# The latents' first norm moved to the end of the context's second group, and weight casts from GpSimd to ScalarE in both context groups

## Chip, cores and metric

The kernel runs on one core of a Trainium2 chip. The metric is device time in microseconds, the median of several executions; one further execution was profiled. VectorE is DVE in the rows, ScalarE ACT, GpSimd POOL, TensorE PE, and SP issues the DMAs.

## What is computed

A block of two layers on 512 latent tokens and 256 context tokens of width 1024, all in float32. Layer 0 mixes by two groups of gated linear recurrences (HGRN2-like "A", GLA-like "B"), both directions, the context first, its final state carried into the latents. Layer 1 is attention. Each has a SwiGLU feed-forward behind it. Cut to what matters here:

```python
u_lat = modulate(x_lat, ng[0], ml[0], ml[1])      # norm, scale and shift
u_ctx = modulate(x_ctx, ng[0], mc[0], mc[1])
a_lat, b_lat, ag_lat, bg_lat = rec_features(u_lat, ...)   # u @ w_in, split
a_ctx, b_ctx, ag_ctx, bg_ctx = rec_features(u_ctx, ...)
def prefix_scan(lat, ctx, reverse):
    o_c, s_c = chunk_gla(q_c, k_c, v_c, g_c, s0)  # the context
    o, _ = chunk_gla(q, k, v, g, s_c)             # the latents, from its state
```

## The kernel before

Activations lie transposed, features on the partitions, in tiles of 128 x 512. Every weight product runs on split operands: a weight block of 128 x 1024 is loaded (`raw`), cast to a high part (`whi`), and the low part is the difference (`wlo`); activations have the same two parts (`uh`, `ul`), and TensorE adds up high x high, high x low and low x high (L180 with the weight stationary, L190 to L192 with the activation stationary). A context product is 24 matmuls of 256 columns.

`wload` (L119 to L135) issues the load, the cast and the subtraction. Which engine casts and which subtracts is looked up in `cfg["hi"]` and `cfg["lo"]`, strings whose letters are used in turn: p for GpSimd (L130), a for ScalarE (L132), d for VectorE (L133); `engines(ph)` sets them for a phase, and a phase that is not in its table has p and d. `raw` has four buffers, `whi` and `wlo` three each.

The stretch of the change, in the order of the program:

- Phase `ra`: the first context group. `rec_group_a(SC, uc)` makes 12 products for group A's two gates and query (evacuated at L696 and L700); `rec_v_group` makes the values with four weight loads (evacuated at L756).
- Merged into its second half is `norm_lat0`, the latents' first norm: `pre_lat` loads x in eight tiles (L109), squares them on ScalarE (L348, L352), adds the squares on GpSimd (L353), makes the reciprocal root (L369 to L373), spreads it over the partitions by TensorE (L376) and multiplies (L611); `norm_mod` scales (L423), adds the shift and rounds to the high part on ScalarE (L424) and makes the low part (L408). These are the operands of all latents' projections.
- Phase `rb`: the second context group. The first product (for the gates of group B, L765 to L772), four products for B's query and key (L780), B's values, and the gates of the output (`rec_group_g`, L793), 17 weight loads. Merged into it are `gla_a(SC)`, the context's scan of group A, and `gla_b_feat(SC)`, the features of B's scan.
- Phase `la`: the latents' first group, merged with the context's scan of B, its output gates and products, and the weights of the modulation.

`gla_a` makes decays of the gates (L946 to L961; the running sum at L820) and then goes, for each direction and pair of chunks, through transposed keys (TensorE L845, ScalarE L847), scores (L223 into a `tr` bank, masked by VectorE at L873), key-value products (L223 into a `kv` bank), states (ScalarE L988 for the first, GpSimd L984, VectorE L990) and outputs (L223 into the one `o` bank, ScalarE L1001 and L1006, VectorE L1008). There are two `tr` and three `kv` banks.

`merge(main, side, ratio)` steps the side generator `ratio` times for each step of the main one. The order so written is a priority only: a scheduler then lays the instructions into each engine's queue, and a planner gives the buffers of the `u` pool. Each engine runs its queue in order.

Of the kernel before, what the change touches and what calls it, by code (L numbers as in the profile page):

```python
# [45 lines left out]
def block_kernel(ctx, tc, plan, xT, cT, vecs, w2, cst, atm, rope, ada, rec_a, rec_v, rec_g, rec_o, qk_w, v_w, wo_w, ff_in, ff_out, out):  # L46
# [17 lines left out]
    def ut(shape, dt=F32, name="u"):  # L64
        return slot(up, "u", shape, dt, name)
# [37 lines left out]
    SL, SC = Stream("l", NT_L), Stream("c", NT_C)  # L103
# [9 lines left out]
    def ch(tiles, st, k):  # L113
        return tiles[k // st.r][:, k % st.r, :]


    cfg = {"hi": "p", "lo": "d", "n": 0, "pri": 0, "evp": 150, "ll": False}
# [107 lines left out]
    def psg():  # L225

        t = rr["tags"][rr["i"] % len(rr["tags"])]
        rr["i"] += 1
        return ps(t)
# [230 lines left out]
    def new_u(st, alloc=None):  # L460
        return tuple([(alloc or ut)([P, st.r, st.nt], F32R, name="u" + n_) for _ in range(st.ntile)] for n_ in "hl")
# [78 lines left out]
    def engines(ph):  # L540
        cfg["pri"] = {}.get(ph, 200)
        cfg["ll"] = ph in []
        cfg["hi"], cfg["lo"] = {'co': ['a', 'ddp'], 'rb': ['p', 'ddp'], 'ci': ['a', 'd'], 'kv': ['a', 'ddp'], 'wo': ['pa', 'd'], 'l0': ['a', 'd'], 'f1': ['a', 'd'], 'lo2': ['p', 'dp'], 'kw': ['a', 'd']}.get(ph, ("p", "d"))

    def drain(*gens):
        for g in gens:
            for _ in g:
                pass

    def seq(*gens):  # L550
        for g in gens:
            yield from g
# [5 lines left out]
    def merge(main, side, ratio):  # L558

        acc = 0.0  # L560
        for _ in main:
            acc += ratio
            while acc >= 1.0:
                acc -= 1.0
                next(side, None)
            yield
        yield from side
# [28 lines left out]
    uc = new_u(SC)  # L596
# [54 lines left out]
    def norm_lat0():  # L651
        if XE == 0:
            yield from pre_lat()
        if 1:
            yield from norm_mod(xl0n, None, G1, ada0[0], 0, ul, FL, st=SL)
        else:
            yield from norm_mod(xl0, xl0n[0], G1, ada0[0], 0, ul, FL)
# [85 lines left out]
    def rec_v_group(st, g, u):  # L743
        f = feats[st.name]
        vs = [ut([P, 512], name="v") for _ in range(st.ntok)]
        if g == 0:
            f.vA = vs
        else:
            f.vB = vs
        for hf in range(2):  # L750
            wh = [wload(rec_v[g, hf, q], 1024) for q in range(2)]
            for tt in range(st.ntok):
                p_ = psg()[:, :256]
                gemm_b(p_, wh, u[0], u[1], st, tt)
                with tc.high_priority(offset=cfg["evp"]):
                    nc.scalar.copy(vs[tt][:, hf * 256 : hf * 256 + 256], p_)  # L756
                if tt % 2:
                    yield

    def rec_group_b(st, u):  # L760
        f = feats[st.name]
        lr = ut([32, st.nt], name="lr")
        p_ = proj_one(st, 16, u)
        with tc.high_priority(offset=cfg["evp"]):
            nc.scalar.copy(lr, p_[0:32])  # L765
        yield
        f.gx = [ut([P, st.r, st.nt], name="gxB") for _ in range(4 // st.r)]
        for h in range(4):
            p_ = psg()[:, : st.nt]
            mm(p_, w2s[:, h * 128 : (h + 1) * 128], lr, start=True, stop=True)  # L770
            with tc.high_priority(offset=cfg["evp"]):
                nc.scalar.activation(ch(f.gx, st, h), p_, AF.Identity, bias=vec("bg2", h, h + 1))  # L772
        yield
        f.qk = [[None, None], [None, None]]
        for s in range(2):
            for m in range(2):
                p_ = proj_one(st, 12 + 2 * s + m, u)
                f.qk[s][m] = ut([P, st.nt], name="qkB")
                with tc.high_priority(offset=cfg["evp"]):
                    nc.scalar.mul(f.qk[s][m], p_, 0.125 if s == 0 else 1.0)  # L780
                yield

    def rec_group_g(st, u):
        f = feats[st.name]
        f.gate = [[ut([P, 512], name="gate") for _ in range(st.ntok)] for _ in range(2)]
        for g in range(2):
            for hf in range(2):
                wh = [wload(rec_g[g, hf, q], 1024) for q in range(2)]
                for tt in range(st.ntok):
                    p_ = psg()[:, :256]  # L790
                    gemm_b(p_, wh, u[0], u[1], st, tt)
                    with tc.high_priority(offset=cfg["evp"]):
                        nc.scalar.copy(f.gate[g][tt][:, hf * 256 : hf * 256 + 256], p_)  # L793
                    if tt % 2:
                        yield
# [223 lines left out]
    def gla_b_feat(st):  # L1019
        f = feats[st.name]  # L1020
        n = st.nch
        qd, kd = [], []
        DL = base.tile([P, 4, n], F32, name=uid("dl"), tag=f"dlB{st.name}")
        BM = base.tile([P, 4, n], F32, name=uid("bm"), tag=f"bmB{st.name}")
        nt4 = 4 // st.r
        tl = [ut([P, st.r, st.nt], name="lsg") for _ in range(nt4)]
        for i in range(nt4):
            nc.scalar.activation(tl[i], f.gx[i], AF.Abs)
            nc.scalar.activation(tl[i], tl[i], AF.Exp, scale=-1.0)
        yield  # L1030
        for i in range(nt4):
            nc.scalar.activation(tl[i], tl[i], AF.Ln, bias=1.0)
        yield
        for i in range(nt4):
            nc.vector.scalar_tensor_tensor(b65(gpad[gi[0] % NG])[:, :, 1:65], v8(f.gx[i], st), 0.0, v8(tl[i], st),
                                           ALU.min, ALU.subtract)
            bx = scan_gate()
            a = ut([P, st.r, st.nt], name="aB")
            for d in range(2):
                i0, i1 = decay(bx, d, H[d])  # L1040
                nc.vector.tensor_sub(v8(a, st)[H[d]], i0, i1)
                edge(bx, d, H[d], flat8(DL, st, i), flat8(BM, st, i))
            q = ut([P, st.r, st.nt], name="EB")
            k = ut([P, st.r, st.nt], name="EiB")
            for r in range(st.r):
                h = i * st.r + r
                hp = H[h % 2]
                for d in range(2):
                    E = ut([P, st.nt], name="exB")[hp]
                    Ei = ut([P, st.nt], name="exiB")[hp]  # L1050
                    follow(gk(st), nc.scalar.activation(E, a[H[d], r, :], AF.Exp, scale=1.0 / 16.0))
                    follow(gk(st), nc.scalar.activation(Ei, a[H[d], r, :], AF.Exp, scale=-1.0 / 16.0))
                    nc.vector.tensor_mul(q[H[d], r, :], E, f.qk[0][h // 2][hp])
                    nc.vector.tensor_mul(k[H[d], r, :], Ei, f.qk[1][h // 2][hp])
            qd.append(q)
            kd.append(k)
            yield
        e = base.tile([P, n, 4], F32, name=uid("ex"), tag=f"exB{st.name}")
        ev = e.rearrange("p c h -> p h c")
        f0, f1 = H  # L1060
        nc.gpsimd.tensor_add(ev[f0, :, 1:n], DL[f0, :, 0 : n - 1], BM[f0, :, 1:n])
        nc.gpsimd.tensor_add(ev[f1, :, 0 : n - 1], DL[f1, :, 1:n], BM[f1, :, 0 : n - 1])
        if "B" in carry:
            D = carry["B"][1]
            nc.gpsimd.tensor_add(ev[f0, :, 0], D[f0, :, SC.nch - 1], BM[f0, :, 0])
            nc.gpsimd.tensor_add(ev[f1, :, n - 1], D[f1, :, 0], BM[f1, :, n - 1])
        else:
            nc.gpsimd.memset(ev[f0, :, 0], 0.0)
            nc.gpsimd.memset(ev[f1, :, n - 1], 0.0)
        nc.scalar.activation(e, e, AF.Exp, scale=1.0 / 16.0)  # L1070
        f.bfeat = (qd, kd, DL, e)
        yield
# [118 lines left out]
    if SH:  # L1191
        order = [(s, h) for s in [2, 0, 1] for h in range(4)]
        n1 = 8
        ga, rest = rec_group_a2(3, norm_lat0(), order, n1)
        drain(seq(ga, rec_v_group(SC, 0, uc)))
    else:
        rest = iter(())
        ga = rec_group_a(SC, uc)
        for i in range(6):
            cfg["pri"] = 0 if i < 4 else 0  # L1200
            next(ga)
        cfg["pri"] = 200
        drain(merge(seq(ga, rec_v_group(SC, 0, uc)), norm_lat0(), 0.7))
    rr["tags"] = ["mm"]
    engines("rb")
    rr["tags"] = ['mm']
    drain(merge(seq(rest, rec_group_b(SC, uc), rec_v_group(SC, 1, uc), rec_group_g(SC, uc)), seq(gla_a(SC), gla_b_feat(SC)), 2.8))
    engines("la")
    adat[0] = 'kv'
    rr["tags"] = ['mm', 'mm', 'kv']  # L1210
# [548 lines left out]
```

## Time and profile before

| | us |
|---|---|
| median of 3 runs (1813.05 to 1815.14) | 1813.13 |
| the profiled execution | 1816.63 |
| its span | 1814.8 |
| TensorE busy in it | 1735.1 |
| VectorE busy | 1067.6 |
| ScalarE busy | 751.0 |
| GpSimd busy | 441.4 |

The span goes from the first instruction to the last; the profiled execution has 1.8 us around it. Busy time of the engines overlaps. The mean granted clock of TensorE is 0.975 of its full level.

### The profile page before, as it was taken

How to read it: one execution, taken by the hardware profiler on the slowest of the kernel's cores; microseconds unless marked ns; L12 is line 12 of the kernel's file. 1: busy time of each engine (PE TensorE's matmuls, PEld its weight loads, DVE VectorE, ACT ScalarE, POOL GpSimd, SP SyncE). 2: the span in 40 equal slices, each digit the busy share in tenths (PEclk: the TensorE clock that was granted, in tenths of full speed). 3: DMA queues.
4: the chain of work that ended last, by engine and by line, in shares of the span. 5: the costliest groups of instructions: out<-in, count | busy, mean ns of one | idle time of the engine just before them, and what ended most of it. 6: DMA issues, size and time to landing. Idle time of an engine off the chain costs nothing. (4 is left out here: it accounts for less than half of the span.)

```text
span 1814.8 us, 27226 instructions
## 1 busy us (share of the span) xinstructions
PE 1735.1 (96%) x10711; PEld 1484.9 (82%) x10711; DVE 1067.6 (59%) x1717; ACT 751.0 (41%) x1314; POOL 441.4 (24%) x460
## 2 busy tenths in 40 slices
PE   6889999999899999999999999799999899999997
PEld 3877778798799989988888888787677898888886
DVE  4986544665777634798643536778855853322336
ACT  3653454344645544542222223434755552222311
POOL 3655412433331004400000002424444400000015
PEclk9989999999899999999999999899999899999999
DMA  9426557311144654576554423311011343233323
GB/s 338 136 86 188 174 180 236 93 49 57 47 140 124 179 171 131 189 252 216 182 162 148 139 73 108 112 37 59 12 48 47 117 129 99 86 94 113 97 66 113
DMA packets 83696, 228.18 MB, mean 126 GB/s; under 512 B 9296, under 2 KB 14160, under 8 KB 83568
## 3 DMA queue, kind: packets, MB, share of 16 engines
q1 hardware_dynamic: 83568, 226.45, 40.0%
q8 instruction: 84, 1.38, 0.3%
q14 instruction: 44, 0.36, 0.1%
HBM read 224.31 MB, written 2.10 MB: 125 GB/s over the span
## 5 line engine op out<-in xcount | busy, mean ns | idle before, releaser
L133 DVE TENSOR_TENSOR wlo<-raw,whi 128x1024 fp32r<-128x1024 f32 (+3 forms) x296 | 359.2, 1215 | 312.6 <-ACT whi L132 228.6
L132 ACT CAST whi<-raw 128x1024 fp32r<-128x1024 f32 (+2 forms) x199 | 201.5, 1014 | 467.3 <-issue 173.4
L130 POOL TENSOR_SCALAR whi<-raw 128x1024 fp32r<-128x1024 f32 (+1 forms) x113 | 121.1, 1074 | 762.3 <-PE ps_mm L180 356.8
L180 PE MATMUL ps_mm<-uh,whi 128*128 128x256 f32 (+1 forms) x840 | 289.3, 345 | 2.3 <-POOL whi L130 2.2
L180 PE MATMUL ps_mm<-uh,wlo 128*128 128x256 f32 (+1 forms) x840 | 286.2, 342 | 2.8 <-DVE wlo L133 2.8
L180 PE MATMUL ps_mm<-ul,whi 128*128 128x512 f32 (+1 forms) x840 | 287.1, 342 | 0.0
L180 PE MATMUL ps_kv<-uh,wlo 128*128 128x512 f32 (+1 forms) x696 | 246.0, 353 | 3.8 <-DVE wlo L133 3.8
L180 PE MATMUL ps_kv<-uh,whi 128*128 128x512 f32 (+1 forms) x696 | 247.7, 356 | 0.0
L180 PE MATMUL ps_kv<-ul,whi 128*128 128x512 f32 (+1 forms) x696 | 246.0, 353 | 0.0
L180 PEld LDWEIGHTS ps_mm<-uh,whi 128*128 128x128 f32 x840 | 161.3, 192 | 24.1 <-POOL whi L130 2.6
L180 PEld LDWEIGHTS ps_mm<-uh,wlo 128*128 128x128 f32 x840 | 160.8, 192 | 20.8 <-DVE wlo L133 3.1
L180 PEld LDWEIGHTS ps_mm<-ul,whi 128*128 128x128 f32 x840 | 161.2, 192 | 17.5 <-issue 0.5
L353 POOL TENSOR_TENSOR acc<-acc,sq 128x256 f32<-128x256 f32 (+1 forms) x79 | 93.4, 1185 | 261.9 <-ACT sq L352 255.8
L180 PEld LDWEIGHTS ps_kv<-uh,whi 128*128 128x128 f32 x696 | 132.7, 191 | 22.5 <-issue 2.9
L180 PEld LDWEIGHTS ps_kv<-uh,wlo 128*128 128x128 f32 x696 | 132.3, 190 | 21.8 <-DVE wlo L133 4.0
L180 PEld LDWEIGHTS ps_kv<-ul,whi 128*128 128x128 f32 x696 | 132.5, 190 | 17.6
L190 PE MATMUL ps_mm<-whi,uh 128*128 128x256 f32 x344 | 103.7, 302 | 8.4 <-ACT gate L793 8.4
L290 DVE SCALAR_TENSOR_TENSOR aacc<-ar,s,aacc 128x512 f32<-128x512 f32 x112 | 81.9, 759 | 34.0 <-DMA ar<-in_ada_dram 33.1
L191 PE MATMUL ps_mm<-wlo,uh 128*128 128x256 f32 x344 | 100.8, 295 | 0.7 <-DVE wlo L133 0.7
L192 PE MATMUL ps_mm<-whi,ul 128*128 128x256 f32 x344 | 100.5, 294 | 0.0
L180 PE MATMUL ps_kv<-hh,whi 128*128 128x512 f32 (+1 forms) x282 | 100.2, 355 | 0.0
L180 PE MATMUL ps_kv<-hh,wlo 128*128 128x512 f32 (+1 forms) x282 | 100.1, 355 | 0.0
(325 smaller groups left out, 3555.0 us busy)
## 6 DMA issues: line engine op xcount, KB each, us to landing
raw<-in_ff_in_dram SPq DMA_DIRECT2D x138, 512.0 KB, 3.7
ar<-in_ada_dram SPq DMA_DIRECT2D x192, 256.0 KB, 4.2
raw<-in_ff_out_dram SPq DMA_DIRECT2D x52, 512.0 KB, 3.5
raw<-in_rec_a_dram SPq DMA_DIRECT2D x34, 512.0 KB, 4.1
raw<-in_rec_v_dram SPq DMA_DIRECT2D x16, 512.0 KB, 3.7
raw<-in_rec_g_dram SPq DMA_DIRECT2D x16, 512.0 KB, 3.7
raw<-in_rec_o_dram SPq DMA_DIRECT2D x16, 512.0 KB, 3.6
raw<-in_wo_w_dram SPq DMA_DIRECT2D x14, 512.0 KB, 3.6
```

The lines of the kernel that those rows point to most:

```text
L130: nc.gpsimd.tensor_scalar(hi[:, :n], raw[:, :n], 1.0, 0.0, ALU.mult, ALU.add)
L132: nc.scalar.copy(hi[:, :n], raw[:, :n])
L133: (nc.gpsimd if cfg["lo"][q % len(cfg["lo"])] == "p" else nc.vector).tensor_sub(lo[:, :n], raw[:, :n], hi[:, :n].bitcast(F32))
L180: mm(ps_, a, b, start=(i == 0), stop=(i == len(q) - 1))
L190: mm(ps, ah, hi[:, s], start=(k == 0), stop=False)
L191: mm(ps, ah, lo[:, s], start=False, stop=False)
L192: mm(ps, al, hi[:, s], start=False, stop=(k == KD - 1))
L290: nc.vector.scalar_tensor_tensor(a, raw, s_, a, ALU.mult, ALU.add)
L353: (nc.vector if i else nc.gpsimd).tensor_add(d, d, q)
```

## The change

The norm goes from the side of `ra` to the end of the side of `rb`, behind the scan and the features of B, and the ratio of that merge from 2.8 to 3.2. The first group runs alone. In `ra` and `rb` the high parts are cast by ScalarE, and all low parts in `rb` are made by VectorE (before, each third by GpSimd).

```diff
-        cfg["hi"], cfg["lo"] = {'co': ['a', 'ddp'], 'rb': ['p', 'ddp'], 'ci': ['a', 'd'],
+        cfg["hi"], cfg["lo"] = {'ra': ['a', 'd'], 'co': ['a', 'ddp'], 'rb': ['a', 'd'], 'ci': ['a', 'd'],
...
-        drain(merge(seq(ga, rec_v_group(SC, 0, uc)), norm_lat0(), 0.7))
+        drain(ga, rec_v_group(SC, 0, uc))
     rr["tags"] = ["mm"]
     engines("rb")
     rr["tags"] = ['mm']
-    drain(merge(seq(rest, rec_group_b(SC, uc), rec_v_group(SC, 1, uc), rec_group_g(SC, uc)), seq(gla_a(SC), gla_b_feat(SC)), 2.8))
+    drain(merge(seq(rest, rec_group_b(SC, uc), rec_v_group(SC, 1, uc), rec_group_g(SC, uc)), seq(gla_a(SC), gla_b_feat(SC), norm_lat0()), 3.2))
```

What this does to the queues, at three places. First ScalarE's queue at the start of the first group, before:

```order
L348 ACTIVATE acc_599<-xl_583 128x512
L352 ACTIVATE sq_601<-xl_585 128x512
L352 ACTIVATE sq_604<-xl_587 128x512
L352 ACTIVATE sq_607<-xl_589 128x512
L352 ACTIVATE sq_610<-xl_591 128x512
L352 ACTIVATE sq_613<-xl_593 128x512
L696 ACT_TABLE_LOAD
L696 ACTIVATE zA_325<-ps_mm_333 128x256
```

and now:

```order
L132 CAST whi_361<-raw_359 128x1024
L424 ACTIVATE uh_98<-nt_153,ada_159 128x256 x2
L132 CAST whi_393<-raw_391 128x1024
L132 CAST whi_425<-raw_423 128x1024
L696 ACT_TABLE_LOAD
L696 ACTIVATE zA_325<-ps_mm_333 128x256
L132 CAST whi_457<-raw_455 128x1024
L696 ACTIVATE zA_325<-ps_mm_365 128x256
L132 CAST whi_489<-raw_487 128x1024
```

The squares of x are gone from here, and a cast stands between one gate's evacuation and the next.

Second, VectorE's queue in the scan of the context around the second score mask (`Tb`), before:

```order
L133 TENSOR_TENSOR wlo_938<-raw_935,whi_937 128x1024
L408 SCALAR_TENSOR_TENSOR ul_113<-nt_768,ada_159,uh_105 128x512
L423 TENSOR_SCALAR nt_902<-nt_902,gv_220 128x512
L408 SCALAR_TENSOR_TENSOR ul_114<-nt_900,ada_159,uh_106 128x512
L423 TENSOR_SCALAR nt_904<-nt_904,gv_220 128x512
L956 TENSOR_TENSOR Ei_1259<-bx_1256 128x512
L873 COPY_PREDICATED Tb_1132<-mk_sb,ps_tr_1133 128x512
L408 SCALAR_TENSOR_TENSOR ul_115<-nt_902,ada_159,uh_107 128x512
```

and now (`lsg` and `gxB` belong to the gates of B, `R` is a state):

```order
L133 TENSOR_TENSOR wlo_1079<-raw_1076,whi_1078 128x1024
L1035 SCALAR_TENSOR_TENSOR gpad_313<-gxB_897,lsg_1481 128x8x64
L873 COPY_PREDICATED Tb_1006<-mk_sb,ps_tr_1007 128x512
L990 TENSOR_TENSOR R_989<-S_987,ps_kv_943 128x512
L820 SCALAR_TENSOR_TENSOR bx_1490<-cst_sb,gpad_313 128x520
L1041 TENSOR_TENSOR aB_1492<-bx_1490 64x512 x2
L1035 SCALAR_TENSOR_TENSOR gpad_314<-gxB_898,lsg_1482 128x8x64
L990 TENSOR_TENSOR R_1059<-S_1057,ps_kv_1047 128x512
```

The norm's passes around the mask are gone; the features of B stand between the masks and state sums instead.

Third, VectorE's queue ahead of the latents' first projection, before (`wlo_1879` is its low weight part):

```order
L1148 TENSOR_TENSOR ob_1089<-ob_1089,gate_1481 128x512
L873 COPY_PREDICATED T_2149<-mk_sb,ps_tr_2151 128x512
L873 COPY_PREDICATED T_2150<-mk_sb,ps_tr_2152 128x512
L1110 TENSOR_TENSOR T_2149<-T_2149,T_2150 128x512
L133 TENSOR_TENSOR wlo_1879<-raw_1876,whi_1878 128x1024
L133 TENSOR_TENSOR wlo_1952<-raw_1949,whi_1951 128x1024
```

and now:

```order
L1148 TENSOR_TENSOR ob_996<-ob_996,gate_1412 128x512
L423 TENSOR_SCALAR nt_1750<-nt_1750,gv_220 128x512
L133 TENSOR_TENSOR wlo_1765<-raw_1762,whi_1764 128x1024
L133 TENSOR_TENSOR wlo_1879<-raw_1876,whi_1878 128x1024
L408 SCALAR_TENSOR_TENSOR ul_111<-nt_1684,ada_159,uh_103 128x512
L423 TENSOR_SCALAR nt_1752<-nt_1752,gv_220 128x512
L408 SCALAR_TENSOR_TENSOR ul_112<-nt_1750,ada_159,uh_104 128x512
L423 TENSOR_SCALAR nt_1754<-nt_1754,gv_220 128x512
L873 COPY_PREDICATED T_2062<-mk_sb,ps_tr_2064 128x512
```

The eight tiles of the norm (`nt`, `ul_111` to `ul_118`) now stand here, between low weight parts and the masks of B's scan.

## Rows read from the trace of the kernel before

**Rows 1.** The page's first part: busy time, share of the span, instructions.

```profile
PE 1735.1 (96%) x10711; PEld 1484.9 (82%) x10711; DVE 1067.6 (59%) x1717; ACT 751.0 (41%) x1314; POOL 441.4 (24%) x460
```

**Rows 2.** Table by stretch: length, busy by engine (count), clock, DMA share, GB/s.

```profile
33.70:98.70 65.00, 55.98 (x432) 54.55 (x433) 61.72 (x74) 43.34 (x59) 40.28 (x36) 0.92 0.54 172
98.70:145.50 46.80, 40.88 (x283) 34.11 (x282) 38.99 (x45) 25.39 (x48) 27.89 (x28) 0.82 0.27 85
145.50:160.00 14.50, 11.36 (x73) 9.52 (x72) 13.43 (x18) 4.90 (x11) 5.82 (x4) 0.88 0.72 219
160.00:244.00 84.00, 84.00 (x531) 65.79 (x529) 39.96 (x50) 34.46 (x56) 35.49 (x34) 1.00 0.59 191
```

**Rows 3.** The same table, a stretch at the lower clock.

```profile
106.60:123.60 17.00, 16.09 (x64) 12.83 (x64) 13.46 (x19) 11.79 (x19) 4.72 (x3) 0.50 0.22 66
```

**Rows 4.** TensorE's waits, 36 to 200 us: total, times, longest.

```profile
PE ps_kv L180 <- DVE wlo L133: 3.8, 1, 3.8
PE ps_tr L223 <- DVE Tb L873: 3.2, 1, 3.2
PE ps_mm L180 <- DVE wlo L133: 2.8, 1, 2.8
PE ps_tr L845 <- DVE EiB L1054: 2.4, 1, 2.4
PE ps_tr L376 <- DVE rs L373: 1.3, 1, 1.3
```

**Rows 5.** Timeline of TensorE (start, duration), 256 columns, then 512.

```profile
72.50 0.28 PE L180 MATMUL ps_kv<-uh,whi 128*128 128x256 f32 x1
...
75.02 0.28 PE L180 MATMUL ps_mm<-uh,whi 128*128 128x256 f32 x1
...
201.25 0.39 PE L180 MATMUL ps_mm<-uh,whi 128*128 128x512 f32 x1
201.48 0.39 PE L180 MATMUL ps_mm<-ul,whi 128*128 128x512 f32 x1
```

**Rows 6.** VectorE by line and shape, 32 to 120 us: busy, mean ns, idle before.

```profile
L133 DVE TENSOR_TENSOR wlo<-raw,whi 128x1024 fp32r<-128x1024 f32 x19 | 26.0, 1371 | 0.0
L408 DVE SCALAR_TENSOR_TENSOR ul<-nt,ada,uh 128x512 fp32r<-128x512 f32 x8 | 8.8, 1102 | 0.0
```

**Rows 7.** GpSimd by line and shape, 38 to 160 us.

```profile
L130 POOL TENSOR_SCALAR whi<-raw 128x1024 fp32r<-128x1024 f32 x23 | 32.2, 1403 | 26.6 <-PE ps_mm L192 6.6 <-PE ps_mm L180 5.3 <-PE ps_kv L180 4.2
L353 POOL TENSOR_TENSOR acc<-acc,sq 128x512 f32<-128x512 f32 x7 | 12.1, 1727 | 3.2 <-ACT sq L352 3.0
L984 POOL TENSOR_TENSOR S<-R,ex 128x512 f32<-128x512 f32 x6 | 8.4, 1399 | 11.9 <-DVE R L990 8.1 <-ACT R L988 3.8
```

**Rows 8.** Timelines of VectorE and GpSimd, single passes.

```profile
101.33 2.87 DVE L408 SCALAR_TENSOR_TENSOR ul<-nt,ada,uh 128x512 fp32r<-128x512 f32 x1
...
101.21 2.44 POOL L133 TENSOR_TENSOR wlo<-raw,whi 128x1024 fp32r<-128x1024 f32 x1
...
107.35 0.73 DVE L408 SCALAR_TENSOR_TENSOR ul<-nt,ada,uh 128x512 fp32r<-128x512 f32 x1
108.01 0.47 DVE L423 TENSOR_SCALAR nt<-nt,gv 128x512 f32<-128x512 f32 x1
...
122.21 1.23 DVE L820 TENSOR_TENSOR_SCAN bx<-cst_sb,gpad 128x520 f32<-128x520 f32 x1
```

**Rows 9.** ScalarE by line and shape: the casts over the span, then 38 to 100 us.

```profile
L132 ACT CAST whi<-raw 128x1024 fp32r<-128x1024 f32 x174 | 183.0, 1052 | 398.8 <-issue 173.4 <-PE ps_kv L180 118.9 <-PE ps_mm L180 90.4
...
L696 ACT ACT_TABLE_LOAD x6 | 7.7, 1283 | 0.1
...
L958 ACT ACTIVATE E<-Ei 128x512 f32<-128x512 f32 x3 | 1.9, 633 | 6.1 <-DVE Ei L956 6.1
```

**Rows 10.** Timeline of ScalarE, a table load and the next activation.

```profile
49.77 1.28 ACT L696 ACT_TABLE_LOAD   x1
51.06 0.38 ACT L696 ACTIVATE zA<-ps_kv 128x256 f32<-128x256 f32 x1
```

More of the change, by code (lines that the diff above doesn't have):

```diff
@@ L542, in engines @@
         cfg["ll"] = ph in []
-        cfg["hi"], cfg["lo"] = {'co': ['a', 'ddp'], 'rb': ['p', 'ddp'], 'ci': ['a', 'd'], 'kv': ['a', 'ddp'], 'wo': ['pa', 'd'], 'l0': ['a', 'd'], 'f1': ['a', 'd'], 'lo2': ['p', 'dp'], 'kw': ['a', 'd']}.get(ph, ("p", "d"))
+        cfg["hi"], cfg["lo"] = {'ra': ['a', 'd'], 'co': ['a', 'ddp'], 'rb': ['a', 'd'], 'ci': ['a', 'd'], 'kv': ['a', 'ddp'], 'wo': ['pa', 'd'], 'l0': ['a', 'd'], 'f1': ['a', 'd'], 'lo2': ['p', 'dp'], 'kw': ['a', 'd']}.get(ph, ("p", "d"))
     def drain(*gens):
```

## The prediction

> **What bounds the kernel now.** I read the engines' shares first. TensorE is busy for 96% of the span [rows 1], so time can only be won where it idles or runs at the lower clock. The table by stretch says where that is. From 33.7 to 160 us, the context's projections and scans, it idles 65.00 - 55.98 = 9.0 us, then 5.9 and 3.1 us, and its mean granted clock is 0.92, 0.82 and 0.88; from 160 to 244 us it never idles and has clock 1.00 [rows 2]. One piece is at the lower level throughout: 106.6 to 123.6 us at 0.50, that is 1.2 GHz instead of 2.4, with 16.09 us busy, so some 8 us of it are lost [rows 3]. At 244.0 us TensorE begins the latents' seventh projection. Up to there both kernels give it the same work, and behind it their orders differ in a few rows only, so I predict when TensorE gets there.
>
> The waits name VectorE: 3.8 and 2.8 us for low weight parts, 3.2 us for a score mask, 2.4 us for a key feature, 1.3 us for the latents' own reciprocal [rows 4]. VectorE is busy 61.72 of the first 65 us [rows 2]: it is what bounds that stretch, and TensorE pays.
>
> **The change, part by part.** My unit is a product, 24 matmuls of 256 columns; 21 of them start 2.52 us apart in all, 0.120 each, so a product is 2.9 us, and a matmul of 512 columns is 0.23 us [rows 5].
>
> *The norm leaves the first group.* Eight low parts of 1.10 us and eight each of two other passes go from VectorE's queue there, and seven additions of 1.73 us from GpSimd's [rows 6, 7]. What stays on VectorE gets shorter too, as GpSimd is quiet: a latents' low part took 2.87 us beside a GpSimd pass of 2.44 us, and 0.73 us without one; a low weight part averages 1.37 us here [rows 6, 8]. The DMAs of x (eight of 256 KB) leave the place between the fourth and the fifth weight load and now stand between the value and gate weights.
>
> *33 casts go from GpSimd to ScalarE*, 16 in the first group and 17 in the second, 1.40 us each there [rows 7] and 1.05 us on ScalarE [rows 9]. Six low parts go from GpSimd to VectorE: 2.44 us there [rows 8], at most 1.37 here [rows 6].
>
> *First group.* The first low part waits 2.8 us [rows 4], behind passes that GpSimd's casts slow; I take 1.5 us off, so that TensorE starts at 37.1 instead of 38.6 us. To the end of the second group's first product it has 406 matmuls, 48.7 us, and 0.8 us of others. Against this stands ScalarE. From the fourth cast on, up to the second group's first cast, it holds 14 casts of 1.05, 13 table loads of 1.28 and 12 activations of 0.63 [rows 9], and eight half-size sigmoids of about 0.4: 42 us, against 350 matmuls or 42.0 us for TensorE in the same part. So ScalarE is full, and its casts come late at the latest point: the second half of the value weights. Walked row by row, TensorE stands there some 2.6 us for a cast, behind which the value evacuations and the exponentials queue. With 2.0 us for the low clock before 41.7 us, which stays, and 1.5 us for one more dip: 37.1 + 49.5 + 2.6 + 2.0 + 1.5 = 92.7 us.
>
> *The scan of the context* (before: 98.7 to 145.5 us). TensorE's work there at full clock was 40.88 - 8.0 = 32.8 us [rows 2, 3]; one product (2.9) now lies ahead of it and the last pair of chunks (3.6) behind, so 26.3 us remain. The chain decides: matmul, ScalarE copy, GpSimd state 1.40 us [rows 7], VectorE sum, matmul. VectorE no longer has the norm between its masks, but it now has the feature work of the gates there, of which the two scans (1.23 us each [rows 8]) wait for logarithms on ScalarE that stand behind table loads of 1.28 us [rows 9]. Walking the rows I find TensorE waiting 1.5 us for the first transposed keys, 3.6 us for the third ones (behind three exponentials), 3.6 us for a bank freed by a state sum that is queued behind the second gate's logarithm, and 2.0 us in small ones: 10.7 us. Gaps of that size went with the lower clock before [rows 3, 4]; I put 5 us for it, less than the 8 before, as the waits absorb a part. 92.7 + 26.3 + 10.7 + 5 = 134.7 us.
>
> *From there to the seventh projection.* Before, 145.5 to 244.0 us was 98.5, less 3.1 idle and 14.5 x 0.12 = 1.7 for the clock [rows 2]: 93.7. Added are the last pair (3.6) and the norm's statistics matmuls (1.4): 98.7 us. VectorE was busy 39.96 of 84 us there [rows 2], so the norm and the six low parts fit in the sum; what is late next is the first latents' projection. From the broadcast of the reciprocals TensorE has 17.5 us of gate products and small matmuls (96 of 0.120, and some 6 us of transposes and scores), then 53 matmuls of 512 columns (12.2 us) in which the eight normed tiles are used one by one: 29.7 us of cover. VectorE starts 2.2 us later, behind a low weight part, and needs 26 us by the undisturbed durations (24 passes of 0.47 to 0.73 us [rows 8], 15 us, five low weight parts, 6, masks and sums between them, 5), 32 by the disturbed means (1.10 for such a pass, 1.37 for a weight part [rows 6]), since GpSimd still casts the latents' weights. So the last tile comes 28 to 34 us after: a wait of 0 to 4.5 us. I take 2.5, and 3 for a dip of the clock behind it: 5.5 us; bounds 0 and 10.
>
> Sum: 134.7 + 98.7 + 5.5 = 238.9 against 244.0: 5.1 us less. The profiled execution takes 1816.6, so 1811.5; it stands 3.5 us above the median of the runs, 1813.1, which gives **1808.0 us**.
>
> One rule speaks against the casts on ScalarE. After a load of 1.28 us the next activation starts 0.01 us after its end [rows 10], so I count 1.28 us a load. The Trainium skill (ScalarE: Activation LUTs, What ACT_TABLE_LOAD costs) counts a drain of some 1.38 us as well, 2.66 us per switch; the 13 loads above would then cost an estimated 18 us more. The trace disagrees.
>
> **The rivals.**
> *More than forecast.* If VectorE's freedom also closes the waits of the scan (10.7 and 5 us come to 5) and the norm's tail is covered, 15 us are won: 1798. For it: four of the five longest waits end on VectorE [rows 4]. Against it: the chain runs over four engines, and the new order puts logarithms and casts into it.
> *Nothing comes of it.* The norm moves from a stretch with 3 us of slack on VectorE to one where the projections wait for it. With the tail at its bound of 10 us the sum is 243.4: 1812.5, no change. It decides if the last tile comes over 34 us behind the broadcast.
> *Slower.* The scan starves TensorE so that all of it runs at 1.2 GHz: ScalarE, a single queue, now holds casts beside every copy of the chain. If VectorE's and GpSimd's steps keep the disturbed durations, the waits grow from 10.7 to 18 us, and of 26.3 us of work at the lower level 15 come on top instead of 5: the scan takes 59 us instead of 42, and the sum is 256: 1825; half of that excess gives 1816.5. It decides at a scan of 42 + 5.1 + 3.6 = 51 us. Before, it was 46.8 [rows 2] with more work in it, which speaks against.
> *A hold behind each table load.* If each of the 13 loads held ScalarE for its own length again (1.28 us [rows 10]), the first group would be 16.6 us longer and the kernel 11.5 us slower, 1824.6. That is the rule above as a mechanism; the row speaks against it.
> That the change does not do what it says is no case: the orders show each part.
>
> **How the numbers follow.** A measurement tells about 0.2% or 3.6 us from no change. Forecast (3.6 to 11 us won) 0.42, more than that 0.16, no change 0.26, the starved scan 0.14, the held loads 0.02. So faster 0.58, same 0.26, slower 0.16. The range leaves out 1 in 10 on each side: the better half of "more" below 1798, and the worse part of the slower cases above 1815.5.
>
> **What would show it.** Right: VectorE well under 95% in the first stretch, TensorE's 3.8 and 1.3 us waits gone, one wait for a ScalarE cast near 82 to 86 us, the first product of the second group ending near 93 us, the scan done near 135, the seventh projection near 239. A wait of the latents' first projection for VectorE near 200 us should be under 5 us. Wrong: TensorE waits for casts all through the first group; a stretch at 0.50 longer than 17 us in the scan; the latents' projections standing over 10 us for the norm; or a gain before 160 us that is gone again by the end of the program.

## The result, and the profile after

The changed kernel takes 1795.63 us (median of 6 runs, 1793.36 to 1802.29), the kernel before beside it 1813.93 (6 runs, 1811.08 to 1816.27): a ratio of 0.9904, with an interval of 0.9886 to 0.9921. It is 1.0% faster, 18 us, where I had forecast 5; the time lies 2.4 us below my range.

The profiled execution took 1795.28 us. The shares of its span (1793.5 us), which answer to [rows 1]:

```profile
PE 1723.8 (96%) x10711; PEld 1477.9 (82%) x10711; DVE 1048.4 (58%) x1723; ACT 773.5 (43%) x1342; POOL 386.0 (22%) x421
```

The table by stretch, against [rows 2, 3]; the columns are length, then TensorE, its weight loads, VectorE, ScalarE and GpSimd busy, then clock, DMA share, GB/s. The first stretch ends with the second group's first product, the second ahead of the second group's values, the last where TensorE begins the latents' seventh projection; the fifth row is the piece at the lower clock (1.2 GHz) in the scan, and the only other one in these stretches ends at 41.28 us:

```profile
33.70:90.95 57.25, 53.65 (x419) 52.74 (x420) 43.82 (x62) 49.70 (x65) 6.11 (x11) 0.94 0.58 169
90.95:128.44 37.49, 32.19 (x237) 28.05 (x235) 23.79 (x32) 26.47 (x48) 10.65 (x16) 0.82 0.36 112
128.44:160.00 31.56, 31.56 (x251) 27.50 (x250) 18.91 (x24) 18.06 (x29) 13.82 (x10) 1.00 0.66 211
160.00:227.47 67.47, 66.89 (x413) 50.00 (x411) 49.57 (x65) 36.04 (x53) 24.85 (x24) 1.00 0.63 203
...
102.70:116.40 13.70, 10.63 (x56) 9.26 (x57) 6.53 (x9) 11.52 (x24) 5.53 (x11) 0.50 0.01 1
```

The seventh projection begins at 227.47 instead of 243.97 us: 16.5 us are won by there and kept. Behind it the two traces differ by another 4.8 us, but the profiled execution of before stood 2.7 us above the median of the six runs; of the 18.3 us between the medians, 1.8 are left for what comes later. VectorE is busy 43.82 of the first 57.25 us, where it was full; GpSimd has 6 us of work left in it. TensorE's waits from 36 to 200 us, against [rows 4]:

```profile
PE ps_kv L223 <- ACT kT L847: 2.9, 1, 2.9
PE ps_kv L190 <- ACT whi L132: 1.6, 1, 1.6
PE ps_kv L223 <- DVE R L990: 1.5, 1, 1.5
PE ps_mm L180 <- ACT whi L132: 1.5, 1, 1.5
PE ps_tr L223 <- DVE T L873: 0.6, 1, 0.6
PE ps_mm L770 <- ACT lr L765: 0.5, 1, 0.5
PE ps_kv L180 <- DVE wlo L133: 0.4, 1, 0.4
PE ps_o L223 <- POOL S L984: 0.3, 1, 0.3
```

The 3.8, 3.2, 2.8, 2.4 and 1.3 us of before are gone; what is left ends mostly on ScalarE. VectorE's passes are shorter, too; the groups that answer to [rows 6], the second one from 34 to 245 us:

```profile
L133 DVE TENSOR_TENSOR wlo<-raw,whi 128x1024 fp32r<-128x1024 f32 x21 | 26.2, 1250 | 6.5 <-ACT whi L132 6.5
...
L408 DVE SCALAR_TENSOR_TENSOR ul<-nt,ada,uh 128x512 fp32r<-128x512 f32 x8 | 5.9, 740 | 0.0
```

VectorE now idles 6.5 us before its low weight parts: it waits for casts instead of being waited for.

### The profile page after: what moved, and what is told of

It is laid out like the page before. It is cut to its first block, busy times and chain, and to the rows that moved or that the text cites. A ratio compares the mean times of both kernels' runs of the same rounds, so it can differ in the third digit from the quotient of the medians.

```text
span 1793.5 us, 27238 instructions
## 1 busy us (share of the span) xinstructions
PE 1723.8 (96%) x10711; PEld 1477.9 (82%) x10711; DVE 1048.4 (58%) x1723; ACT 773.5 (43%) x1342; POOL 386.0 (22%) x421
## 5 line engine op out<-in xcount | busy, mean ns | idle before, releaser
L133 DVE TENSOR_TENSOR wlo<-raw,whi 128x1024 fp32r<-128x1024 f32 (+3 forms) x302 | 365.6, 1213 | 298.2 <-ACT whi L132 235.5
L132 ACT CAST whi<-raw 128x1024 fp32r<-128x1024 f32 (+2 forms) x232 | 235.2, 1015 | 478.9 <-issue 176.1
L180 PE MATMUL ps_mm<-ul,whi 128*128 128x256 f32 (+1 forms) x840 | 287.2, 342 | 0.0
L180 PE MATMUL ps_mm<-uh,wlo 128*128 128x512 f32 (+1 forms) x840 | 286.9, 342 | 0.0
L130 POOL TENSOR_SCALAR whi<-raw 128x1024 fp32r<-128x1024 f32 (+1 forms) x80 | 79.1, 991 | 727.1 <-PE ps_mm L180 349.3
L180 PE MATMUL ps_kv<-hl,whi 128*128 128x512 f32 (+1 forms) x282 | 100.0, 355 | 0.0
```

What stands on the lines that cost most here:

```text
L130: nc.gpsimd.tensor_scalar(hi[:, :n], raw[:, :n], 1.0, 0.0, ALU.mult, ALU.add)
L132: nc.scalar.copy(hi[:, :n], raw[:, :n])
L133: (nc.gpsimd if cfg["lo"][q % len(cfg["lo"])] == "p" else nc.vector).tensor_sub(lo[:, :n], raw[:, :n], hi[:, :n].bitcast(F32))
L180: mm(ps_, a, b, start=(i == 0), stop=(i == len(q) - 1))
```

## The experiments

**The parts, apart.** The change has three: the norm's move (with the ratio), the casts of the first group (`ra`), and the casts and low parts of the second (`rb`). Theory V is my prediction's: the norm's load on VectorE was the cost. Rival G: GpSimd's casts were, as they stretch VectorE's passes. Rival B: only both together pay.

The norm alone:

```diff
-        {'ra': ['a', 'd'], 'co': ['a', 'ddp'], 'rb': ['a', 'd'],
+        {'co': ['a', 'ddp'], 'rb': ['p', 'ddp'],
```

> The norm is moved and the ratio is 3.2, as in the change; both groups keep the casts of before (GpSimd casts, in the second group each third low part by GpSimd). Theory V (VectorE's load in the first group was what TensorE paid for; the norm's passes leaving is the gain): 10 to 16 us faster than before, 1798 to 1804; VectorE under 85% busy from 34 to 92 us, no long wait for a low weight part there. Theory G (GpSimd's casts were what stretched VectorE's passes; the gain is the casts' move): the low weight parts still take about 1.37 us beside GpSimd's casts and the gain is at most 5 us, 1808 to 1813. Theory B (each alone leaves one of them in the way, only both together pay): 0 to 5 us here and 0 to 5 us with the casts alone.

Measured 1811.29 us against 1813.96; ratio 0.9986, interval 0.9970 to 1.0001. The casts alone:

```diff
-        drain(ga, rec_v_group(SC, 0, uc))
+        drain(merge(seq(ga, rec_v_group(SC, 0, uc)), norm_lat0(), 0.7))
...
-    drain(merge(seq(...), seq(gla_a(SC), gla_b_feat(SC), norm_lat0()), 3.2))
+    drain(merge(seq(...), seq(gla_a(SC), gla_b_feat(SC)), 2.8))
```

> All casts of both context groups by ScalarE and all low parts by VectorE as in the change, but the norm stays beside the first group and the ratio at 2.8. Theory V: VectorE stays full in the first group (its 24 passes of the norm are still there), gain 0 to 5 us, 1808 to 1813. Theory G: VectorE's passes take 0.5 to 1.2 us instead of 0.9 to 1.4, the waits for low parts go, gain 10 to 16 us, 1797 to 1803. Theory B: 0 to 5 us. A rival on the other side: ScalarE, which then has the norm's squares and the casts in one queue, lets TensorE wait for casts in the first group by over 5 us, and the time is 1815 to 1825.

Measured 1803.02 us; ratio 0.9932, interval 0.9910 to 0.9955. The norm with one of the two cast parts, first without `rb`, then without `ra`:

```diff
-        'rb': ['a', 'd'],
+        'rb': ['p', 'ddp'],
```

> The change without its part on the second group: there GpSimd casts and makes each third low part as before. If the second group's casts are worth nothing (GpSimd has room there): within 3 us of the change, 1793 to 1799. If GpSimd's casts beside the scan slow VectorE's masks and state sums: the scan of the context takes 40 to 47 us instead of 37.5, and the time is 1799 to 1806. If ScalarE's casts stand in the way of the scan's copies (my prediction's worry), this is faster than the change by 2 to 4 us, 1790 to 1793.

Measured 1803.93 us; ratio 0.9939, interval 0.9917 to 0.9962.

```diff
-        {'ra': ['a', 'd'], 'co': ['a', 'ddp'],
+        {'co': ['a', 'ddp'],
```

> The change without its part on the first group: there GpSimd casts as before. By my prediction's account ScalarE is full in the first group with its casts, so giving them back removes the 1.65 us wait for a cast but slows VectorE's low parts: within 3 us of the change, 1793 to 1799. If GpSimd's casts stretch VectorE's low parts to 1.37 us so that TensorE waits for them, the first group ends 2 to 6 us later than 90.95 and the time is 1798 to 1803.

Measured 1802.00 us; ratio 0.9933, interval 0.9911 to 0.9956. Theory V falls: the norm alone is not told from nothing, the casts alone bring some 11 of the 18 us. That is also more than rival B allowed; both numbers lie where rival G put them. The timelines of TensorE say where (us; the first group's end is that of its last value matmul, and the norm's few statistics matmuls move with it):

| | first group ends | from there to the 7th projection | 7th projection begins |
|---|---|---|---|
| before | 98.90 | 145.07 | 243.97 |
| norm alone | 92.07 | 148.49 | 240.56 |
| casts alone | 94.66 | 134.68 | 229.34 |
| norm, `ra` | 87.39 | 144.50 | 231.89 |
| norm, `rb` | 92.83 | 139.74 | 232.57 |
| the change | 88.07 | 139.40 | 227.47 |

Each row is one execution. That of the casts alone was the fastest of its six, 5.1 us below their median, so its row shows the casts at their best: the norm's part beside them is 1.9 us in the table and 7.4 between the medians, whose intervals overlap.

In the first group the two add up: the norm's going brings 6.8 us, the casts 4.2, both 10.8. Behind it the norm's coming costs 3.4 us with the casts of before and 4.7 with the new ones; the casts bring 10.4 us without the norm and 9.1 with it, of which `rb` alone has 8.8 (and 5.1 on top of `ra`). So the norm gives half of its gain or more back, and the larger part of what the casts bring lies behind the first group, where my sum gave their move no gain.

What the casts of `rb` did shows in the kernel with the norm alone, whose longest single wait (TensorE at 131.24 us, 4.9 us) was not there before and is not there in the change. It ends on an evacuation by ScalarE (`qkB`, L780), and that is queued behind a square which waits for VectorE's sum `ob`:

```profile
136.15 0.58 PE L190 MATMUL ps_mm<-whi,uh 128*128 128x256 f32 x1 [4.91 <-ACT qkB L780]
...
135.20 0.63 ACT L913 ACTIVATE osq<-ob 128x512 f32<-128x512 f32 x1 [6.44 <-DVE ob L1008]
```

VectorE there:

```profile
127.11 2.06 DVE L133 TENSOR_TENSOR wlo<-raw,whi 128x1024 fp32r<-128x1024 f32 x1
129.09 5.35 DVE L1054 TENSOR_TENSOR EiB<-exiB,qkB 64x256 f32<-64x256 f32 x4
134.47 0.69 DVE L1008 TENSOR_TENSOR ob<-ob,ps_o 128x512 f32<-128x512 f32 x1
...
136.81 1.71 DVE L1054 TENSOR_TENSOR EiB<-exiB,qkB 64x256 f32<-64x256 f32 x4
```

and GpSimd beside it:

```profile
128.06 2.02 POOL L130 TENSOR_SCALAR whi<-raw 128x1024 fp32r<-128x1024 f32 x1
130.02 0.53 POOL L872 MEMSET T<- 128x512 f32 x1
130.51 1.19 POOL L130 TENSOR_SCALAR whi<-raw 128x1024 fp32r<-128x1024 f32 x1
131.78 2.38 POOL L133 TENSOR_TENSOR wlo<-raw,whi 128x1024 fp32r<-128x1024 f32 x1
```

The first set of four key features takes 5.35 us while GpSimd works (to 134.16), the second, of the same shape, 1.71 us when it has stopped. One by one, the first four are:

```profile
129.09 1.25 DVE L1054 TENSOR_TENSOR EiB<-exiB,qkB 64x256 f32<-64x256 f32 x1
130.36 0.42 DVE L1054 TENSOR_TENSOR EiB<-exiB,qkB 64x256 f32<-64x256 f32 x1
130.79 1.17 DVE L1054 TENSOR_TENSOR EiB<-exiB,qkB 64x256 f32<-64x256 f32 x1
131.97 2.47 DVE L1054 TENSOR_TENSOR EiB<-exiB,qkB 64x256 f32<-64x256 f32 x1
```

The second runs beside the memset, which reads nothing, and takes its undisturbed 0.42 us. The other three each end 0.27 or 0.28 us after the cast or subtraction beside them: they stood until GpSimd's pass was done. In the changed kernel both sets take 1.71. The kernel with the norm and `ra` has its first set at 5.35 us and the same wait of 4.9; the one with the norm and `rb` has neither.

**Is it the pass on GpSimd, or the lateness of its casts?** Three kernels leave ScalarE's casts as in the change and add passes on GpSimd whose result nobody reads, at each of the 33 weight loads. The first, with short passes that read and write a scratch tile:

```diff
+            if cfg.get("x"):
+                gA = cfg["x"]
+                nc.gpsimd.tensor_scalar(gA[:, 0:8], raw[:, 0:8], 1.0, 0.0, ALU.mult, ALU.add)
+                for _ in range(4):
+                    nc.gpsimd.tensor_scalar(gA, gA, 1.0, 0.0, ALU.mult, ALU.add)
```

> The changed kernel, and beside it, at each of the 33 weight loads of the two context groups, five passes on GpSimd that nobody waits for: one of 128x8 that waits for the load, and four of 128x256 that read and write a scratch tile. ScalarE still makes the casts. Theory P (a GpSimd pass that reads SBUF holds up VectorE's passes that have two SBUF inputs, and this, not the lateness of GpSimd's casts, was their cost): VectorE's low weight parts go from about 1.2 to 1.4 us or more in the first group, and the time from about 1796 to 1799 to 1808. Rival L (GpSimd's casts cost through their own lateness and queue, VectorE merely follows): within 2 us of the change, 1793 to 1798, and VectorE's passes as in the change.

Measured 1821.93 us; ratio 1.0046, interval 1.0029 to 1.0063: slower than before, beyond both expectations. VectorE's low weight parts went from 1.22 to only 1.27 us (34 to 100 us). The added passes took 0.66 us each, and GpSimd was busy 50 of the 56 us from 34 to 90 us. Its own small steps stood in that queue: ScalarE waited 4.2 us for one of them (`ex`) with a cast behind it, and TensorE 3.5 us for that cast. This kernel measured its side effect; between the theories it decides nothing.

The control, with passes that only write:

```diff
-                    nc.gpsimd.tensor_scalar(gA, gA, 1.0, 0.0, ALU.mult, ALU.add)
+                    nc.gpsimd.memset(gA, 0.0)
```

> The same, but the four passes of 128x256 only write the scratch tile (memset) and read nothing. They occupy GpSimd for about as long. Theory P: passes that only write do not hold up VectorE's two-input passes; within 2 us of the change, 1793 to 1798, though GpSimd is as busy as with the reading passes. If any GpSimd activity slows VectorE: as late as with the reading passes, 1799 to 1808. Rival L: within 2 us of the change as well.

Measured 1802.82 us; ratio 0.9936, interval 0.9921 to 0.9950. That is some 6 to 7 us slower than the change. The time lies in the range of "any GpSimd activity", its mechanism does not: VectorE's two-input passes are as in the change, the low weight parts 1.22 us in the first group. (Passes that scale one SBUF input, L951 of the change, are a little longer there, 0.55 us instead of 0.43.) TensorE's new waits are 1.7 us for GpSimd's states (L984 of the change, 0.3 there) and 2.7 us for a weight load of the modulation; SP, which issues those loads, waits 10.5 us for the added passes from 34 to 245 us, where in the change it waits 6.4 us for GpSimd's sums. GpSimd's own queue runs late. Part of that may lie in the short pass at each load, which makes GpSimd wait for the load; no run has the writing passes without it. Then one long reading pass per load, as long as a cast, writing 8-bit values:

```diff
+            if cfg.get("x"):
+                nc.gpsimd.tensor_scalar(cfg["x"], raw, 1.0, 0.0, ALU.mult, ALU.add)
```

> The changed kernel; at each of the 33 weight loads of the two context groups GpSimd also makes one pass of 128x1024 that reads the loaded weights and writes an 8-bit scratch tile that nobody reads (as long a reading pass as the casts of before). ScalarE still makes the casts. The writing passes of the run before are the control: GpSimd's own queue is then late (1802.8), VectorE's low weight parts stay at 1.22 us. Theory P: VectorE's low weight parts take 1.35 us or more in the first group, its passes with one input in PSUM stay at 0.68 to 0.73, and the time is 1804 to 1812. Rival L: low weight parts as in the change, 1793 to 1803.

Measured 1807.07 us; ratio 0.9959, interval 0.9943 to 0.9975, which overlaps the control's by a little, so that the reading costs more than the writing is likely and not shown by the times. VectorE by line and shape from 34 to 245 us, first with the long reading passes:

```profile
L135 DVE TENSOR_TENSOR wlo<-raw,whi 128x1024 fp32r<-128x1024 f32 x42 | 59.6, 1428 | 7.9 <-ACT whi L134 6.7 <-POOL whi L132 1.1
...
L1058 DVE TENSOR_TENSOR EiB<-exiB,qkB 64x256 f32<-64x256 f32 x8 | 4.9, 616 | 0.1
L410 DVE SCALAR_TENSOR_TENSOR ul<-nt,ada,uh 128x256 fp32r<-128x256 f32 x6 | 4.3, 753 | 0.0
...
L994 DVE TENSOR_TENSOR R<-S,ps_kv 128x512 f32<-128x512 f32 x6 | 4.1, 681 | 5.9 <-POOL S L988 5.9
```

then with the writing ones:

```profile
L138 DVE TENSOR_TENSOR wlo<-raw,whi 128x1024 fp32r<-128x1024 f32 x42 | 56.2, 1343 | 8.4 <-ACT whi L137 7.3 <-POOL whi L135 0.9
...
L998 DVE TENSOR_TENSOR R<-S,ps_kv 128x512 f32<-128x512 f32 x6 | 4.1, 682 | 6.8 <-POOL S L992 6.8
L1062 DVE TENSOR_TENSOR EiB<-exiB,qkB 64x256 f32<-64x256 f32 x8 | 3.3, 418 | 0.1
```

and in the change:

```profile
L133 DVE TENSOR_TENSOR wlo<-raw,whi 128x1024 fp32r<-128x1024 f32 x42 | 55.4, 1324 | 9.9 <-ACT whi L132 8.7 <-POOL whi L130 1.1
...
L990 DVE TENSOR_TENSOR R<-S,ps_kv 128x512 f32<-128x512 f32 x6 | 4.1, 680 | 3.7 <-POOL S L984 3.7
L1054 DVE TENSOR_TENSOR EiB<-exiB,qkB 64x256 f32<-64x256 f32 x8 | 3.3, 418 | 0.1
L408 DVE SCALAR_TENSOR_TENSOR ul<-nt,ada,uh 128x256 fp32r<-128x256 f32 x6 | 2.6, 477 | 0.0
```

(The lines are shifted by the added code: L135 and L138 are L133, L994 and L998 are L990, L1058 and L1062 are L1054, L410 is L408.) With reading passes on GpSimd the VectorE passes beside them that have two inputs from SBUF (low parts, key features) are longer; the state sum, which has one input in PSUM, takes 0.68 us in all three. In the first group alone (34 to 90 us) the low weight part is 1.343 against 1.219 us; I had said 1.35 or more. So both theories hold a part: reading passes slow VectorE, and what GpSimd has in its queue makes its own states late.

The Trainium skill (SBUF — State Buffer, Who interferes with whom) says just this: a VectorE instruction with two SBUF inputs contends with a GpSimd instruction that reads SBUF, not with one that only writes it, and one of them stands still meanwhile; with at most one SBUF input (outside some faster modes) it does not. These runs agree: 5.35 against 1.71 us, 0.68 us throughout, and 0.42 and 1.22 us beside the writing passes. Two inputs are not the whole of it, though. The passes that scale the gates (L951) read one tile from SBUF, and they too were longer in the kernel before; shortest, median and longest, in ns, there and in the change:

```profile
L951 DVE TENSOR_SCALAR zA<-zA x12: 408/428/1300, 49.8 to 326.7; 128x512 f32<-128x512 f32 x12
...
L951 DVE TENSOR_SCALAR zA<-zA x12: 398/427/433, 50.2 to 310.2; 128x512 f32<-128x512 f32 x12
```

Whether such a faster mode is the reason no run shows.

**The tail, and the order on the side.** The ratio back at 2.8, `norm_lat0()), 2.8))`:

> The changed kernel with the merge's ratio back at 2.8. The norm and the features of group B come later in the second group. If the norm's tail was as close as my prediction had it (cover 29.7 us against 28 to 34), the latents' first projection now waits 3 to 8 us for the norm, 1798 to 1804. If there is room: within 2 us of the change, 1793 to 1798.

Measured 1796.92 us; ratio 0.9906, interval 0.9887 to 0.9924, which is not told from the change: there is room. The norm ahead of the features of B, `seq(gla_a(SC), norm_lat0(), gla_b_feat(SC))`:

> The changed kernel with the norm ahead of the features of group B on the side of the second group instead of behind them. If the norm's late place costs TensorE something in front of the latents' first projection (the 3 to 5 us that the kernels with the moved norm are longer behind the first group), this is 2 to 4 us faster than the change: 1791 to 1794. If the features of B are what TensorE needs first: their matmuls wait instead, 1798 to 1805. If both fit: 1794 to 1798.

Measured 1800.24 us; ratio 0.9917, interval 0.9896 to 0.9937. That is not better; the interval overlaps the change's, so whether it is worse stays open.

**Further along the same way.** The next phase's casts by ScalarE, `'la': ['a', 'd']` added to the table:

> The changed kernel with the next phase's casts (the latents' first group) by ScalarE as well. TensorE waits 0.6 us in all there in the changed kernel, so if only waits of TensorE count, nothing changes: 1793 to 1798. If GpSimd's quiet is worth something in itself (fewer delays handed on to later phases): 2 to 5 us faster, 1790 to 1793. If ScalarE's queue, with the casts in front of the gates' evacuations, becomes the bound there: 3 to 8 us slower, 1798 to 1804.

Measured 1792.81 us; ratio 0.9879, interval 0.9861 to 0.9896, which overlaps the change's. All phases but `wo`:

```diff
-        cfg["hi"], cfg["lo"] = {'ra': ['a', 'd'], 'co': ['a', 'ddp'],
...
+        cfg["hi"], cfg["lo"] = {'wo': ['pa', 'd']}.get(ph, ("a", "d"))
```

> The changed kernel with every phase's high parts cast by ScalarE and all low parts made by VectorE, but for the phase of the attention's output weights, which stays. If what counts is GpSimd's reading passes beside a VectorE that TensorE waits for: those waits are gone already in the two context groups and elsewhere the waits are for table loads, reciprocals and softmax; 1788 to 1796, about as with the next phase alone (1792.8). If ScalarE becomes late in the feed-forwards and the attention: 1797 to 1810.

Measured 1788.75 us (4 runs, 1787.28 to 1789.53); ratio 0.9858, interval 0.9835 to 0.9881, clear of the change's: the best of the kernels run, 25 us below before. Its engines:

```profile
PE 1720.5 (96%) x10711; PEld 1472.2 (82%) x10711; DVE 1038.9 (58%) x1733; ACT 842.1 (47%) x1428; POOL 289.6 (16%) x327
```

From 34 to 245 us TensorE waits more than in the change (14.9 against 9.1 us in waits over 0.4 us), and its seventh projection begins 3.2 us later, at 230.63; the gain lies behind that, where waits over 0.5 us, from 245 us on, come to 27.9 instead of 36.7. ScalarE, at 47%, had the room. The same with the norm back beside the first group and the ratio at 2.8:

> The kernel of the run before it (all casts by ScalarE, all low parts by VectorE), with the norm back beside the first group and the ratio at 2.8. Once GpSimd's reading passes are gone everywhere, is the norm's move worth anything? If the norm moved is worth what the traces of casts alone and of the whole change show up to the latents' seventh projection (229.3 against 227.5): 2 us slower than the 1788.75 of that kernel, 1789 to 1792. If it is worth the 7 us between the medians of casts alone and the whole change: 1794 to 1797. If the move is a loss where GpSimd is quiet: 1784 to 1788.

Measured 1794.75 us; ratio 0.9910, interval 0.9886 to 0.9935, against 0.9858: with GpSimd's casts gone nearly everywhere the norm's move (with its ratio) is worth some 6 us. With GpSimd's casts in place it was worth none that can be told.

## Why the prediction was wrong, step by step

The direction and the place were right: VectorE relieved, TensorE fed, the gain made before the seventh projection and kept. The sum came to 238.9 us there, against 227.47: 11.4 us too late, in three terms, 1.7, 4.5 and 5.2 us. In size this is the rival "more than forecast" (15 us won), to which I had given 0.16, but that it comes so near is luck. Its covered tail is there; waits and clock in the scan come to 10.6 us where it had 5; and its 15 us left the tail's 5.5 out: 5.1, 10.7 and 5.5 make 21.3, or 1791.8 us. The lower end of my range, 1798, stood on that slip. (I also read four of the five longest waits in [rows 4] as ending on VectorE; all five do.)

*First group*, 92.7 forecast, 90.95 measured. The first low part's wait went altogether: the matmul that stood 2.84 us for it before and started at 38.62 starts at 36.51, where I had 37.1. It would be earlier but for the second cast, for which TensorE waits 1.50 us now that ScalarE makes it, 0.77 before. The later wait for a cast is where I put it and shorter, 1.65 us for 2.6:

```profile
81.29 0.28 PE L192 MATMUL ps_mm<-whi,ul 128*128 128x256 f32 x1
83.22 0.39 PE L190 MATMUL ps_kv<-whi,uh 128*128 128x256 f32 x1 [1.65 <-ACT whi L132]
```

The extra dip of the clock that I priced at 1.5 us did not come: behind the one that ends at 41.28 us the granted clock is full up to the scan. ScalarE, which I called full, was: from its fourth cast to the second group's first (42.73 to 83.06 us) it is busy for 39.63 of 40.33 us. TensorE still waits for it only that once there. Its loads hold nothing beyond their own 1.28 us, so that rival is out:

```profile
80.04 1.28 ACT L947 ACT_TABLE_LOAD   x1
81.33 0.63 ACT L947 ACTIVATE gpad<-zA 128x512 f32<-128x512 f32 x1
```

*The scan*, 42.0 forecast, 37.5 measured. This is the step that failed in size: "TensorE waiting 1.5 us for the first transposed keys, 3.6 us for the third ones (behind three exponentials), 3.6 us for a bank freed by a state sum that is queued behind the second gate's logarithm, and 2.0 us in small ones: 10.7 us". In its place TensorE idles for 37.49 - 32.19 = 5.3 us. For the first transposed keys it does not wait at all; there are 2.9 us for the third ones, 1.5 us for the state sum, and 0.8 us in small ones (the copy `lr`, L765, and a state of GpSimd). Behind the third keys' exponentials ScalarE reads:

```profile
102.10 0.42 ACT L1051 ACTIVATE exB<-aB 64x256 f32<-64x256 f32 x1 [1.80 <-DVE aB L1041]
102.42 0.83 ACT L1052 ACTIVATE exiB<-aB 64x256 f32<-64x256 f32 x2
103.27 0.58 ACT L847 COPY kT<-ps_tr 128x512 f32<-128x512 f32 x1
```

and the state sum stands behind the second gate's logarithm, as I said, for less time:

```profile
107.53 0.69 DVE L1035 SCALAR_TENSOR_TENSOR gpad<-gxB,lsg 128x512 f32<-128x512 f32 x1 [4.70 <-ACT lsg L1032]
108.14 0.68 DVE L990 TENSOR_TENSOR R<-S,ps_kv 128x512 f32<-128x512 f32 x1
```

I had laid whole durations end to end. Here a pass of 0.42 us is followed by the next one 0.32 us after its start. Added up over the chain ahead of the third keys, such overlaps are some 0.4 us of the 0.7 missing there; why the state sum comes 2.1 us earlier than I had it no run shows. Disturbed passes were not gone from the chain, either: the difference of two decays (`aB`) that the first exponential waits for takes 1.34 us beside GpSimd's state, and 0.68 in the kernel with the casts alone, where GpSimd stood still:

```profile
100.72 1.34 DVE L1041 TENSOR_TENSOR aB<-bx 64x512 f32<-64x512 f32 x1
...
99.67 1.85 POOL L984 TENSOR_TENSOR S<-R,ex 128x512 f32<-128x512 f32 x1 [2.89 <-PE ps_o L223]
```

The clock's 5 us came out: 10.63 us of matmuls at 0.50, 5.3 lost. But I had them for 10.7 us of waits, and half of those came, so the sum is not a confirmation of how I got there.

*The tail*, 5.5 forecast for the latents' first projection, 0.6 measured (the 0.6 us for `T` in the list, and no dip of the clock). The last normed tile was ready at 189.44 us, 28.1 after the broadcast's end at 161.31, the lower of my two bounds (28 to 34): all eight low parts took their undisturbed 0.74 us. The first matmul that reads it starts at 192.66, so 3.2 us were to spare. My cover was about right (31.3 us for 29.7). Taking the middle between the disturbed and the undisturbed durations was the fault. GpSimd still casts there, but only three times in these 28 us, busy for 7.83 of them, and it met three scaling passes (1.26 to 1.28 us instead of 0.47) and one low weight part (2.05 us), none of the norm's low parts. The ratio at 2.8 costs nothing that can be told, either.

*What was not in the sum.* I charged the slow passes beside GpSimd to the first group alone, and in "slower" let every step of the scan keep its disturbed duration. Masks and state sums have none in these traces (one input in PSUM, 0.67 to 0.75 us). The passes that do, the features of B, the low parts and the scalings, stand in and behind the scan too, and there the casts' going was worth more in the traces than in the first group. Run apart, the casts bring some 11 of the 18 us and the norm, which I had put first, under 3, not told from nothing.

## What to carry to other kernels

Where VectorE is what TensorE waits for, look at what GpSimd does at those moments before counting VectorE's passes: a set of two-input passes took three times as long here (5.35 for 1.71 us), and moving GpSimd's reading passes to an engine with room (here ScalarE, 43%) can be worth more than moving VectorE's own work. Price the moved work with the durations that hold beside what still runs there, and walk a chain by the starts of its passes, not by durations laid end to end. A move may pay only in company, as the norm's did: take one back at a time.

## What the runs showed of the hardware

Three VectorE forms told apart by their inputs beside the same GpSimd work: `EiB` (two from SBUF) 1.17 to 2.47 us beside a reading pass and 0.42 beside a memset or nothing; `ob` and `R` (one from PSUM) 0.69 and 0.68 us in either case; L951 (one from SBUF, scaled) up to 1.30 us against 0.43. GpSimd pays as well. Its timeline in the run with short reading passes, two sets of the same four, the first beside a scan, a low part and two decays on VectorE. One by one the first set's passes take 1.21, 1.43, 0.72 and 0.72 us, and each ends 0.20 to 0.26 us after the VectorE pass that was under way when it began:

```profile
60.52 4.32 POOL L133 TENSOR_SCALAR gsA<-gsA 128x256 f32<-128x256 f32 x4
...
65.21 1.86 POOL L133 TENSOR_SCALAR gsA<-gsA 128x256 f32<-128x256 f32 x4
```

And an engine off the critical path was not free: writing passes (33.5 us of them from 34 to 135 us), each set behind a short pass that waits for a load, on a GpSimd that had 6 us of work left in the first group cost 6 to 7 us, and TensorE's new waits end on GpSimd's own later steps and on a load.
